# Splitting the queries as whole tiles: rows moved by DMA, the sink's column on ScalarE

## The chip, the cores and the metric

The kernel runs on one core of one Trainium2 chip. The metric is the device time of one execution in microseconds, the median of the runs shown. The engines are TensorE (PE, with its weight loads PEld), VectorE (DVE), ScalarE (ACT), GpSimd (POOL) and SyncE (SP), whose queue issues the DMAs.

## The reference, cut to what matters

Two layers of a hybrid block on 1024 tokens of width 1024. Each layer: RMSNorm; one projection to queries (16 heads of 64), keys and values (2 heads of 64), the two inputs of a convolution and two gates; attention with a window of 128 and learned sinks; a causal depthwise convolution of width 31 with LayerNorm; a gated merge and an output projection; then a SwiGLU feed-forward block. All in float32. The part that the change touches:

```
q = partial_rope(rmsnorm(q, q_norm), cos, sin)      # per head of 64
s = einsum('bnqkgd,bnskd->bnkgqs', qb, kb) * scale  # blocks of 128 queries, 256 keys
m = max(max(s), sink);  p = exp(s - m)
p = p / (sum(p) + exp(sink - m));  o = p @ vb
```

## The kernel before, in words

Everything is kept transposed, channels on partitions and the 1024 tokens along the row. A float32 product is made of three products of reduced-precision parts (F32R): a value x is split into a high part (a cast by ScalarE) and a low part (x minus the high part, by VectorE or GpSimd), and high x high, high x low and low x high are summed in PSUM (`mm3`, line 236). Weights are loaded by SP (`fetch`, L125), cast by ACT (L133) and subtracted by POOL (L134).

In each layer `INPROJ` lists 34 column tiles of the input projection; each takes eight steps of six matmuls, and after every step `tick()` runs the events that are due by then. So attention, the convolution's taps (L496 on VectorE) and the normalisations are laid between the projection's matmuls at fixed steps. The order of PE and, in this part, of DVE is the order in which the program writes its instructions; that of ACT, POOL and SP is chosen by the framework's planner from a model of times, and every engine then works its queue in order.

A query tile holds a pair of heads, head 0 on partitions 0 to 63 and head 1 on 64 to 127. `queries` (L581) evicts it to `q32`, squares it for the norm, and rotates it: `rope` has four small DMAs that shift rows into `rot`, POOL multiplies, DVE adds (L400). `split`, seven steps after the projection, then fills two tiles `qs[0]` and `qs[1]`, one per head, both 128 partitions high: the head's high part on its own 64 partitions, its low part on the other 64. As a key tile `kh` holds the same key rows on both halves, one matmul of 128 rows multiplies high and low part of a head at once. The high halves are two ACT copies (L609), the low halves two DVE subtracts (L613), which read one half of the partitions and write the other.

Sixteen steps after the first query tile the attention units begin, one per six steps: unit (i, j) takes pair i and two blocks of queries. `unit_s` (L622) makes the scores in the PSUM tile `S` (one buffer; L633, L634), puts the sink's column beside them (POOL copy L636 of `sr`, which DVE makes in L599), and copies the rest by ACT (L638); `top` masks (DVE L643, L645), takes the maximum (L649, L651) and the exponentials (ACT L653); `norm` divides (L658, L660). `unit_t` transposes on PE (L669), `masks` selects on POOL (L681, L684), `unit_o` multiplies with the values in the PSUM tile `po` (L699), which the head norm (L391, L394) uses too. PE can write `S` again when L638 and L645 have read it, and `po` when L394 or L711 have.

Tiles tagged `t4` share four buffers of 128x1024: `q32`, `sqh`, the convolution's inputs, the gates.

Of the kernel before, what the change touches and what calls it, by code (L numbers as in the profile page):

```python
# [12 lines left out]
F32 = mybir.dt.float32  # L13
F32R = mybir.dt.float32r
U32 = mybir.dt.uint32
AF = mybir.ActivationFunctionType
ALU = mybir.AluOpType
# [4 lines left out]
P = 128  # L22
# [5 lines left out]
HD = 64  # L28
# [24 lines left out]
def trunk(ctx, tc, xT, win, wcv, wout, wgu, wdn, vecs, cosT, sinT, outT):  # L53
    nc = tc.nc

    def pool(name, bufs=1, space=None, stack=None, side=None):
        kw = dict(name=name, bufs=bufs, reuse_waits="tile")
        if side is not None:
            kw["side"] = side
        if space is not None:  # L60
            kw["space"] = space
        if space is DRAM:
            kw.pop("reuse_waits")
        return (stack or ctx).enter_context(tc.tile_pool(**kw))
# [136 lines left out]
    def next_p():  # L201
        ahead(PAHEAD)
        return pieces.pop(0)


    clock = [0]
# [3 lines left out]
    def at(when, fn):  # L210
        heapq.heappush(events, (when, next(serial), fn))

    def after(n, fn):
        at(clock[0] + n, fn)
# [4 lines left out]
    def when_free(bank, n, fn):  # L219
        def go():  # L220
            if bank in busy:
                after(0.25, go)
            else:
                fn()
        after(n, go)
# [41 lines left out]
    def t4(name):  # L267
        return tp.tile([P, T], F32, tag="t4", bufs=T4, name=name)
# [52 lines left out]
    for l in range(DEPTH):  # L321
        vl = vec[l]

        def V(c, n=1):
            return vl[:, c:c + n]
# [54 lines left out]
        def rope(src):  # L380
            for h in range(2):
                o = h * HD
                nc.sync.dma_start(rot[o:o + 8], src[o + 8:o + 16])
                nc.sync.dma_start(rot[o + 8:o + 16], src[o:o + 8])
            nc.gpsimd.tensor_tensor(out=src, in0=src, in1=ct, op=ALU.mult)
            nc.gpsimd.tensor_tensor(out=rot, in0=rot, in1=st_, op=ALU.mult)

        def headnorm(sq, f):
            pss = ps_o("pssh")
            for b in range(NB):  # L390
                nc.tensor.matmul(pss[:, 2 * b:2 * b + 2], sq[:, b * P:(b + 1) * P], blk1,  # L391
                                 start=True, stop=True)
            ssb = sm.tile([P, NB, 2], F32, tag="ssb", name="ssb")
            nc.vector.tensor_tensor(out=ssb, in0=pss[:, 0:16].rearrange("p (b h) -> p b h", h=2),  # L394
                                    in1=e64.unsqueeze(2).broadcast_to([P, NB, 2]), op=ALU.add)
            nc.gpsimd.tensor_tensor(out=f, in0=ssb.rearrange("p b h -> p (b h)"), in1=mhalf, op=ALU.pow)
            return ssb

        def rope_add(src):
            nc.vector.tensor_tensor(out=src, in0=src, in1=rot, op=ALU.add)  # L400
# [178 lines left out]
        qready = {}  # L579

        def queries(i, ps):  # L581
            q32 = t4("q32")
            nc.scalar.activation(q32, ps, AF.Copy, scale=V(V_GQ))
            sq = t4("sqh")
            nc.scalar.activation(sq, ps, AF.Square)
            rope(q32)
            fq = sm.tile([P, 16], F32, tag="fq", bufs=3, name="fq")
            nfq = sm.tile([P, 16], F32, tag="nfq", bufs=3, name="nfq")
            sr = sm.tile([P, NB, 2], F32, tag="sr", bufs=3, name="sr")
            qs = [ap_.tile([P, T], F32R, tag="qs", bufs=QSB, name=f"qs{h}") for h in range(2)]  # L590

            def norm():
                ssb = headnorm(sq, fq)

                def finish():
                    nc.vector.tensor_scalar(out=nfq, in0=fq, scalar1=-1.0, scalar2=None, op0=ALU.mult)
                    nc.vector.tensor_tensor(out=sr.rearrange("p b h -> p (b h)"),
                                            in0=ssb.rearrange("p b h -> p (b h)"), in1=fq, op=ALU.mult)
                    nc.vector.tensor_tensor(  # L599
                        out=sr, in0=sr,  # L600
                        in1=V(V_SK + 2 * i, 2).unsqueeze(1).broadcast_to([P, NB, 2]), op=ALU.mult)
                after(5, finish)

            def split():
                rope_add(q32)
                for h in range(2):
                    hi = slice(h * HD, (h + 1) * HD)
                    lo = slice((1 - h) * HD, (2 - h) * HD)
                    nc.scalar.copy(qs[h][hi], q32[hi])  # L609
                for h in range(2):  # L610
                    hi = slice(h * HD, (h + 1) * HD)
                    lo = slice((1 - h) * HD, (2 - h) * HD)
                    after(1.5 + h, lambda hi=hi, lo=lo, h=h: nc.vector.tensor_tensor(  # L613
                        out=qs[h][lo], in0=q32[hi], in1=qs[h][hi].bitcast(F32), op=ALU.subtract))
            when_free('po', QN, norm)
            after(QSP, split)
            at(clock[0] + QSP + 3.2, lambda: qready.update({i: (fq, nfq, sr, qs)}))


        Av = {}  # L620
# [1 line left out]
        def unit_s(i, j):  # L622
            fq, nfq, sr, qs = qready[i]
            hk = i // 4
            if j == 0:
                Av[i] = ap_.tile([P, T], F32, tag="A", bufs=AB, name="A")
            S = psm.tile([P, 4, 2 * P], F32, tag="S", bufs=1, name="S")
            for n in range(4):
                b, h = 2 * j + n // 2, n % 2
                qb = qs[h][:, b * P:(b + 1) * P]  # L630
                c0 = P if b == 0 else 0
                ks = slice(b * P - P + c0, (b + 1) * P)
                nc.tensor.matmul(S[:, n, c0:], qb, kh[hk][:, ks], start=True, stop=False)  # L633
                nc.tensor.matmul(S[:, n, c0:], qb, kl[hk][:, ks], start=False, stop=True)  # L634
            sc = ap_.tile([P, 4, P + 1], F32, tag="sc", bufs=SCB, name="sc")
            nc.gpsimd.tensor_copy(sc[:, :, P], sr[:, 2 * j:2 * j + 2].rearrange("p b h -> p (b h)"))  # L636
            f0 = 2 if j == 0 else 0
            nc.scalar.copy(sc[:, f0:, 0:P], S[:, f0:, P:])  # L638
            den = sm.tile([P, 4], F32, tag="den", bufs=3, name="den")

            def top():
                if j == 0:
                    nc.vector.tensor_tensor(out=sc[:, 0:2, 0:P], in0=S[:, 0:2, P:],  # L643
                                            in1=mneg.unsqueeze(1).broadcast_to([P, 2, P]), op=ALU.add)
                nc.vector.copy_predicated(  # L645
                    sc[:, f0:, 0:P], mprev.bitcast(U32).unsqueeze(1).broadcast_to([P, 4 - f0, P]),
                    S[:, f0:, 0:P])
                mx = sm.tile([P, 4], F32, tag="mx", name="mx")
                nc.vector.tensor_reduce(out=mx, in_=sc, axis=AX.X, op=ALU.max)  # L649
                nm = sm.tile([P, 4], F32, tag="nm", name="nm")  # L650
                nc.vector.tensor_tensor(out=nm, in0=mx, in1=nfq[:, 4 * j:4 * j + 4], op=ALU.mult)  # L651
                for n in range(4):
                    nc.scalar.activation(sc[:, n], sc[:, n], AF.Exp, bias=nm[:, n:n + 1],  # L653
                                         scale=fq[:, 4 * j + n:4 * j + n + 1], accum_out=den[:, n:n + 1])

            def norm():
                ri = sm.tile([P, 4], F32, tag="ri", name="ri")
                nc.vector.reciprocal(ri, den)  # L658
                for n in range(4):
                    nc.scalar.activation(sc[:, n, 0:P], sc[:, n, 0:P], AF.Copy, scale=ri[:, n:n + 1])  # L660
            after(T1, top)
            after(T2, norm)
            when_free('pT', TD, lambda: unit_t(i, j, sc))

        def unit_t(i, j, sc):
            busy.add('pT')
            pt = ps_pT("pT").rearrange("p (n q) -> p n q", n=4)
            for n in range(4):
                nc.tensor.transpose(pt[:, n], sc[:, n, 0:P], ident)  # L669
            ph = ap_.tile([P, 4, P], F32R, tag="ph", bufs=1, name="ph")  # L670
            nc.scalar.copy(ph, pt)
            pl = ap_.tile([P, 4, P], F32R, tag="pl", bufs=1, name="pl")
            after(0.6, lambda: masks(i, j, pt, ph, pl))
# [276 lines left out]
        for f in FORD[:NCL]:  # L950
# [4 lines left out]
            for m in range(2):  # L955
                bs = [bank(), bank()]
                held.append(bs)
                for kk in range(2):
                    a = next_p()
# [11 lines left out]
        fq = pool("fq", 1, None, fst)  # L971
# [120 lines left out]
        for n, (name, _, _) in enumerate(DOWN):  # L1092
# [3 lines left out]
            for p in range(NG - fl):  # L1096
                w, a = next_p(), next_p()
# [49 lines left out]
QSP = 7  # L1147
# [72 lines left out]
```

## Time and profile before

| what | value |
|---|---|
| time, median of 3 runs | 2714.76 us (2712.35 to 2716.32) |
| profiled execution | 2710.93 us |
| its span, first to last instruction | 2709.2 us |
| PE busy | 2585.2 us, 95% |
| PE weight loads busy | 2112.5 us, 78% |
| DVE busy | 1876.9 us, 69% |
| ACT busy | 1196.4 us, 44% |
| POOL busy | 1654.0 us, 61% |
| mean granted PE clock | 0.979 of full speed |

The profile is of one execution. "Busy" is a union over the whole span, and stages with different limits are mixed in it; the stages have to be read one by one. A duration of an instruction includes time in which it has begun but cannot go on. Idle time of an engine is put down to the instruction whose end released it.

### The profile page before, as it was taken

To read this page: it belongs to the slowest core of one execution; us is meant where nothing else is said; L and a number is where in the kernel's file an instruction comes from. 1 tells how busy PE (TensorE), PEld (TensorE's weight loads), DVE (VectorE), ACT (ScalarE), POOL (GpSimd) and SP (SyncE) were. 2 spreads that over 40 slices of the span, in tenths; PEclk is the share of its full clock that TensorE was granted. 3 is DMA by queue.
4 is the path that set the end of the run, shared out by engine and by line. 5 is a ranking of instruction groups with operands and counts; after the bars stand their busy time and mean duration, and the time that the engine had idled before them with its cause. 6 is when DMAs were issued, how large, how long until landed. Compare 5 with 4: busy or idle time off the path is not lost. (4 is left out here: it accounts for less than half of the span.)

```text
span 2709.2 us, 33260 instructions
## 1 busy us (share of the span) xinstructions
PE 2585.2 (95%) x11736; PEld 2112.5 (78%) x11736; DVE 1876.9 (69%) x2053; ACT 1196.4 (44%) x2251; POOL 1654.0 (61%) x1092
## 2 busy tenths in 40 slices
PE   7898898999999999999999989899999999999999
PEld 5777777888787888878877767778887788888887
DVE  6689999652468777855637999995616668778344
ACT  2266566843432323344523665668325222223443
POOL 7368787535356777764535778785252677767544
PEclk8999999999999999999999999999999999999999
DMA  3111111375244454476711111114752444455666
GB/s 129 42 51 34 57 64 51 140 264 215 86 165 149 170 179 156 160 276 218 239 57 43 41 57 49 59 63 156 251 202 97 175 167 145 163 179 191 223 224 210
DMA packets 132359, 379.06 MB, mean 140 GB/s; under 512 B 15136, under 2 KB 15392, under 8 KB 132192
## 3 DMA queue, kind: packets, MB, share of 16 engines
q1 hardware_dynamic: 132048, 376.85, 40.6%
q8 instruction: 92, 1.51, 0.2%
q14 instruction: 75, 0.61, 0.1%
q10 hardware_dynamic: 144, 0.09, 0.0%
HBM read 259.17 MB, written 115.34 MB: 138 GB/s over the span
## 5 line engine op out<-in xcount | busy, mean ns | idle before, releaser
L151 POOL TENSOR_TENSOR plo<-fraw,phi 128x512 fp32r<-128x512 f32 x290 | 423.0, 1467 | 229.2 <-ACT phi L149 214.7
L151 POOL TENSOR_TENSOR plo<-fs,phi 128x512 fp32r<-128x512 f32 x160 | 264.3, 1663 | 253.5 <-ACT phi L149 241.7
L496 DVE SCALAR_TENSOR_TENSOR y<-a,vec,y 128x1024 f32<-128x1024 f32 x240 | 405.7, 1690 | 4.0
L134 POOL TENSOR_TENSOR wl<-raw,wh 128x1024 fp32r<-128x1024 f32 (+1 forms) x100 | 252.4, 2525 | 241.7 <-PE ps L242 196.6
L149 ACT CAST phi<-fraw 128x512 fp32r<-128x512 f32 x444 | 257.6, 618 | 246.4 <-POOL plo L151 131.8
L242 PE MATMUL ps<-hx,wh 128*128 128x512 f32 x1056 | 349.1, 412 | 7.3 <-ACT hx L283 7.3
L242 PE MATMUL ps<-hx,wl 128*128 128x512 f32 x1056 | 335.8, 399 | 4.4 <-POOL wl L134 4.4
L242 PE MATMUL ps<-lx,wh 128*128 128x512 f32 x1056 | 338.0, 401 | 0.8 <-DVE lx L284 0.8
L149 ACT CAST phi<-fs 128x512 fp32r<-128x512 f32 x160 | 95.4, 620 | 534.3 <-DVE fs L164 529.1
L151 DVE TENSOR_TENSOR plo<-fraw,phi 128x512 fp32r<-128x512 f32 x154 | 133.6, 873 | 187.8 <-ACT phi L149 185.5
L847 PE MATMUL b<-plo,phi 128*128 128x512 f32 x616 | 240.8, 391 | 3.9 <-DVE plo L151 3.6
L242 PEld LDWEIGHTS ps<-hx,wl 128*128 128x128 f32 x1056 | 204.8, 194 | 50.0 <-POOL wl L134 4.8
L242 PEld LDWEIGHTS ps<-lx,wh 128*128 128x128 f32 x1056 | 206.1, 195 | 47.9 <-DVE lx L284 1.6
L847 PE MATMUL b<-phi,plo 128*128 128x512 f32 x616 | 239.8, 389 | 0.0
L847 PE MATMUL b<-phi 128*128 128x512 f32 x616 | 239.7, 389 | 0.0
L242 PEld LDWEIGHTS ps<-hx,wh 128*128 128x128 f32 x1056 | 195.6, 197 | 42.9 <-ACT hx L283 7.3
L653 ACT ACTIVATE sc<-sc,nm,fq 128x129 f32<-128x129 f32 x256 | 123.7, 486 | 118.0 <-DVE nm L651 117.6
L133 ACT CAST wh<-raw 128x1024 fp32r<-128x1024 f32 (+1 forms) x100 | 98.2, 982 | 166.0 <-PE ps L242 128.3
L915 POOL TENSOR_TENSOR g<-g,u 128x512 f32<-128x512 f32 (+1 forms) x84 | 129.4, 1558 | 31.9 <-DVE u L968 25.5
L911 DVE TENSOR_TENSOR g<-g 128x512 f32<-128x512 f32 x88 | 102.0, 1159 | 65.7 <-POOL g L915 42.5
L847 PEld LDWEIGHTS b<-plo,phi 128*128 128x128 f32 x616 | 115.6, 188 | 31.6 <-DVE plo L151 7.6
L847 PEld LDWEIGHTS b<-phi 128*128 128x128 f32 x616 | 115.6, 188 | 24.2
(254 smaller groups left out, 6219.2 us busy)
## 6 DMA issues: line engine op xcount, KB each, us to landing
fraw<-wgu SPq DMA_DIRECT2D x88, 512.0 KB
raw<-win SPq DMA_DIRECT2D x68, 512.0 KB
act<-g SPq DMA_DIRECT2D x44, 512.0 KB
dw<-wdn SPq DMA_DIRECT2D x44, 512.0 KB
td<-g SPq DMA_DIRECT2D x44, 512.0 KB
sd<-dw SPq DMA_DIRECT2D x44, 512.0 KB
fraw<-sd SPq DMA_DIRECT2D x88, 256.0 KB
fraw<-td SPq DMA_DIRECT2D x88, 256.0 KB
```

The lines of the kernel that those rows point to most:

```text
L133: nc.scalar.copy(wh, raw)
L134: nc.gpsimd.tensor_tensor(out=wl, in0=raw, in1=wh.bitcast(F32), op=ALU.subtract)
L149: nc.scalar.copy(hi, src)
L151: (eng or nc.gpsimd).tensor_tensor(out=lo, in0=src, in1=hi.bitcast(F32), op=ALU.subtract)
L242: nc.tensor.matmul(ps[:, sl], a[:, wc], b[:, sl], start=first and j == 0, stop=last and j == 2)
L496: nc.vector.scalar_tensor_tensor(out=y, in0=a[:, j:j + T], scalar=V(w0 + j), in1=y, op0=ALU.mult, op1=ALU.add)
L653: nc.scalar.activation(sc[:, n], sc[:, n], AF.Exp, bias=nm[:, n:n + 1], scale=fq[:, 4 * j + n:4 * j + n + 1], accum_out=den[:, n:n + 1])
L847: nc.tensor.matmul(ps, w[:, ai * P:(ai + 1) * P], x, start=first and j == 0, stop=last and j == 2, skip_group_check=True)
L911: nc.vector.tensor_tensor(out=o, in0=x, in1=y, op=ALU.subtract)
L915: nc.gpsimd.tensor_tensor(out=g[:, sl], in0=g[:, sl], in1=u[:, sl], op=ALU.mult)
```

## The change

The high part of a pair is now one ACT copy of the whole 128x1024 tile into a new `t4` tile `qhi`, and the low part one DVE subtract of the whole tile, written over `q32`. Four DMAs on SP's queue, each of 64 rows of 4 KB from SBUF to SBUF, then bring the rows to `qs[0]` and `qs[1]`: per head the high rows to its own half and the low rows to the other. The subtract stands where the first of the two stood (1.5 steps after `split`); the second is gone. The step at which a pair is entered as ready is put later; it sets no order. Apart from that the sink's column (L636) is copied by ACT instead of POOL.

```
             def split():
                 rope_add(q32)
-                for h in range(2):
-                    ...
-                    nc.scalar.copy(qs[h][hi], q32[hi])
-                for h in range(2):
-                    ...
-                    after(1.5 + h, lambda hi=hi, lo=lo, h=h: nc.vector.tensor_tensor(
-                        out=qs[h][lo], in0=q32[hi], in1=qs[h][hi].bitcast(F32), op=ALU.subtract))
+                hi = t4("qhi")
+                nc.scalar.copy(hi.bitcast(F32R), q32)
+
+                def low():
+                    nc.vector.tensor_tensor(out=q32.bitcast(F32R), in0=q32, in1=hi, op=ALU.subtract)
+
+                    for h in range(2):
+                        r, o = (slice(a * HD, (a + 1) * HD) for a in (h, 1 - h))
+                        q = qs[h].bitcast(F32)
+                        nc.sync.dma_start(q[r], hi[r])
+                        nc.sync.dma_start(q[o], q32[r])
+                after(1.5, low)
             when_free('po', QN, norm)
             after(QSP, split)
-            at(clock[0] + QSP + 3.2, lambda: qready.update({i: (fq, nfq, sr, qs)}))
+            at(clock[0] + QSP + 5, lambda: qready.update({i: (fq, nfq, sr, qs)}))
...
-            nc.gpsimd.tensor_copy(sc[:, :, P], sr[:, 2 * j:2 * j + 2].rearrange("p b h -> p (b h)"))
+            nc.scalar.copy(sc[:, :, P], sr[:, 2 * j:2 * j + 2].rearrange("p b h -> p (b h)"))
```

## Rows read from the trace of the kernel before

**Rows 1.** Stages: start:end and length, busy us of PE, PEld, DVE, ACT, POOL; clock, DMA.
```profile
185.00:240.00 55.00, 49.73 (x246) 42.01 (x247) 53.73 (x60) 34.12 (x78) 43.13 (x28) 0.91 0.14 41
600.00:720.00 120.00, 115.64 (x507) 94.40 (x505) 39.81 (x39) 37.18 (x46) 49.98 (x24) 1.00 0.42 156
```
**Rows 2.** Waits of PE: line, whom it waited for, total us, times, longest.
```profile
PE S L633 <- DVE sc L645: 38.5, 16, 5.0
PE po L699 <- DVE ssb L394: 27.1, 8, 4.7
```
**Rows 3.** Timeline of PE in layer 0: start, duration, instruction, [idle before, releaser].
```profile
118.33 0.33 PE L633 MATMUL S<-kh,qs 128*128 128x128 f32 x1
...
132.51 0.55 PE L633 MATMUL S<-kh,qs 128*128 128x256 f32 x1 [5.04 <-DVE sc L645]
...
169.82 0.33 PE L633 MATMUL S<-kh,qs 128*128 128x128 f32 x1 [1.65 <-DVE sc L645]
...
185.54 0.36 PE L633 MATMUL S<-kh,qs 128*128 128x256 f32 x1 [3.67 <-DVE sc L645]
...
471.40 0.55 PE L699 MATMUL po<-mo,vv 128*128 128x256 f32 x1 [4.60 <-DVE ssb L394]
```
**Rows 4.** Timeline of DVE, first and second pair of heads.
```profile
113.00 2.70 DVE L613 TENSOR_TENSOR qs<-q,qs 64x1024 fp32r<-64x1024 f32 x1
...
117.05 1.22 DVE L613 TENSOR_TENSOR qs<-q,qs 64x1024 fp32r<-64x1024 f32 x1
...
161.44 4.54 DVE L613 TENSOR_TENSOR qs<-q,qs 64x1024 fp32r<-64x1024 f32 x2
...
169.04 0.72 DVE L645 COPY_PREDICATED sc<-mprev,S 128x512 f32<-128x512 uint32 x1
...
183.90 0.81 DVE L492 TENSOR_SCALAR y<-a,vec 128x1024 f32<-128x1024 f32 x1 [3.99 <-DMA yd<-y]
```
**Rows 5.** Groups by line and form: count, busy us, mean ns, idle before them.
```profile
L613 DVE TENSOR_TENSOR qs<-q,qs 64x1024 fp32r<-64x1024 f32 x32 | 74.5, 2327 | 0.9
...
L636 POOL COPY sc<-sr 128x4 f32<-128x4 f32 x64 | 53.2, 833 | 68.9 <-PE pT L669 41.1 <-DVE sr L599 27.7
...
L653 ACT ACTIVATION_READ_ACCUMULATOR sc<-sc,nm,fq 128x1 f32 x256 | 47.9, 187 | 0.0
...
L609 ACT CAST qs<-q 64x1024 fp32r<-64x1024 f32 x32 | 33.5, 1046 | 25.3 <-DVE q L400 25.0
...
L400 DVE TENSOR_TENSOR q<-q,rot 128x1024 f32<-128x1024 f32 x16 | 19.5, 1217 | 2.5 <-POOL rot L386 2.5
```
**Rows 6.** Stage table for line 613 alone, third pair: DVE busy, clock, DMA.
```profile
205.00:230.00 25.00, 6.64 (x2) 0.87 0.07 22
```
**Rows 7.** Timeline of POOL, first and second pair.
```profile
102.68 2.40 POOL L385 TENSOR_TENSOR q<-q,ct 128x1024 f32<-128x1024 f32 x1 [3.91 <-DMA rot<-q]
...
160.30 3.37 POOL L134 TENSOR_TENSOR wl<-raw,wh 128x1024 fp32r<-128x1024 f32 x1
...
167.99 1.18 POOL L636 COPY sc<-sr 128x4 f32<-128x4 f32 x1 [1.51 <-DVE sr L599]
```
**Rows 8.** Waits of POOL before the sink's column.
```profile
POOL sc L636 <- PE pT L669: 41.1, 10, 9.1
...
POOL sc L636 <- DVE sr L599: 27.7, 16, 4.2
```
**Rows 9.** Timeline of SP's queue, 95 to 240 us: start and time of each issue.
```profile
99.60 0.62 SPq L384 DMA_DIRECT2D rot<-q  x1
...
164.08 0.43 SPq L767 DMA_DIRECT2D sB<-g  x1
178.86 0.33 SPq L125 DMA_DIRECT2D raw<-win  x1
179.94 0.33 SPq L503 DMA_DIRECT2D yd<-y  x1
```
**Rows 10.** Chain that ended last: start, us, what (a load of 256 KB).
```profile
2679.55 6.26 DMA x<-xs
```

More of the change, by code (lines that the diff above doesn't have):

```diff
@@ L605, in split @@
                 rope_add(q32)
-                for h in range(2):
-                    hi = slice(h * HD, (h + 1) * HD)
-                    lo = slice((1 - h) * HD, (2 - h) * HD)
-                    nc.scalar.copy(qs[h][hi], q32[hi])
-                for h in range(2):
-                    hi = slice(h * HD, (h + 1) * HD)
-                    lo = slice((1 - h) * HD, (2 - h) * HD)
-                    after(1.5 + h, lambda hi=hi, lo=lo, h=h: nc.vector.tensor_tensor(
-                        out=qs[h][lo], in0=q32[hi], in1=qs[h][hi].bitcast(F32), op=ALU.subtract))
+                hi = t4("qhi")
[8 more added lines that the diff above has]
+                after(1.5, low)
             when_free('po', QN, norm)
             after(QSP, split)
-            at(clock[0] + QSP + 3.2, lambda: qready.update({i: (fq, nfq, sr, qs)}))
+            at(clock[0] + QSP + 5, lambda: qready.update({i: (fq, nfq, sr, qs)}))
         Av = {}
```

## The prediction

> **What bounds the kernel now.** I read the table of stages first. In the stages of layer 0 with attention (185 to 240 us) DVE is busy 53.73 of 55 us, PE only 49.73 and at a granted clock of 0.91; in the block after it (600 to 720) PE has 115.64 of 120 and DVE a third [rows 1]. So the projections with attention, to about 480 us and in the like stretch of layer 1, are bound by DVE, the rest mostly by PE. The list of PE's waits agrees: 38.5 us in 16 waits for the copy that empties the score bank S (L645), 27.1 us in 8 for the tiny L394 that empties the other bank [rows 2]. Neither op is long; each stands at the end of a full DVE queue. PE's timeline shows where: 5.04 us at 132.51, 1.65 at 169.82, 3.67 at 185.54, the last of the layer 4.60 at 471.40 [rows 3]. DVE's timeline of the pair of heads before 169.82 shows the queue: two L613 subtracts from 161.44 on, small ops and taps, L645 ending at 169.76, after which PE starts at once; the only idle stretch is 3.99 us at 183.90, for a store that DVE's own last tap had triggered, so it moves with DVE [rows 4]. In such a stretch a microsecond less on DVE is a microsecond less in the kernel, as long as PE still waits.
>
> **The change, part by part.**
>
> *Half subtracts.* 32 subtracts of 64x1024 take 74.5 us, 2.33 on average [rows 5]; 16 of 128x1024 take their place. The number of partitions costs DVE no time: the rope's add of 128x1024 takes 1.22 us on average (L400) [rows 5], and so does a half subtract at its shortest (117.05) [rows 4]. So the new one takes what one old one took, and one falls away per pair. Its price lies between two ends, neither below nothing, as it leaves a full queue. Alone it is 1.22 us; beside a large POOL op it is 2.70 (113.00), and in one pair the two took 6.64, or 3.3 each [rows 4, 6]. The first of a pair runs into POOL's wl subtract (160.30 to 163.67 beside 161.44) [rows 4, 7]; the new one sits at that same place in DVE's order and keeps that collision. I take 1.22 for the one removed, as in most pairs: where it took more, POOL's op will meet the tap behind it. The last pair of a layer pays nothing, since its subtract stands behind the layer's last wait for DVE at 471.40 [rows 3]. 14 pairs x 1.22 = 17.1 us; the upper end is the whole difference, 16 x (4.65 - 2.70 to 3.3), about 22 to 31 us.
>
> *High parts.* ACT's two half copies (1.05 us each [rows 5]) become one: 16.8 us less on ACT, which has 34.12 of 55 us busy [rows 1]. Worth 0; the copy still ends before DVE comes to the subtract.
>
> *The sink's column.* 64 POOL copies go, 53.2 us, 0.83 each [rows 5], up to 1.18 for four columns [rows 7], more waiting than work. DVE gets at most a start earlier on a few ops, or meets POOL's next op sooner: between -3 and +3, I take 0. On ACT each costs between 0.19 (its accumulator read, one column) and 1.05 (L609) [rows 5]; I take 0.2, as four columns are nearest to one: 13 us, less than the 16.8 that left, and at 1.05 the 50 more would still fit into ACT's idle 21 of 55. POOL idled 41.1 us before this copy for PE's transposes and 27.7 for DVE's sr [rows 8]; in ACT's order these waits now stand in front of exponentials, weight casts and evictions. I take 0, since L638, which follows on ACT, fills the same buffer and has the same wait, and sr is done before the unit's matmuls; if not, it is the second rival.
>
> *The four transfers.* 64 in all, 256 KB each, SBUF to SBUF, on SP's queue. The trace has no such transfer. Issue: 0.43 us for a store (164.08), 0.62 for the small shifts of rot (99.60) [rows 9], so 4 x 0.43 to 0.62 = 1.7 to 2.5 us of SP per pair. From issue to use: rot, 32 KB, issued at 99.60, is read at 102.68: 3.1 us; the 512 KB store yd issued at 179.94 releases DVE at 183.90: 4.0; the worst of 256 KB, in the crowded last stage, is 6.26 [rows 4, 7, 9, 10]. I take 4.0, because the stage is as quiet as at yd, and 0.4 for one issue ahead of it, as the two high parts can leave while DVE still subtracts: 4.4 us from the subtract's end to qs (3.1 to 8.8 at the ends).
>
> Where does that fall? Pair 1: the new subtract ends at 161.44 + 4.54 - 1.22 = 164.76, qs lands at 169.2. S comes free at 169.76 - 1.22 = 168.5. So PE starts at 169.2 and not 169.82, with half of the gain, and the rest is had at 185.54, where DVE alone decides and its queue has run 1.22 earlier all along. Pair 0 has no room: its subtract ends at 115.70, qs lands at 120.1, and the second head was read at 118.33 [rows 3]; PE loses some 2 us there. The wait of 5.04 at 132.51 takes them in, since DVE sets its end and has a full queue until then; without that cover they would cost 2 x 2 us.
>
> What is behind the new waits: SP, in order, holds the four issues until DVE is done. The weight load behind them (or ahead: it left just before 164.08, released by POOL's wl at 163.67) may be 1 to 3 us later; the load after it leaves only at 178.86, so a projection lies in between [rows 7, 9]. The t4 tiles: one more of four is held from the copy to the landing; beside it are q32, at times the held ur and one gate tile, and sqh is free by then. Four fit; nothing is charged.
>
> [...]
>
> Sum: -17 us. The profiled execution took 2710.93 us (span 2709.2), 3.8 less than the median of 2714.76; the same step off the median gives 2698.
>
> **Rivals.**
> 1. More: the removed subtract is worth its average, and POOL, freer, gets in DVE's way less: -25 to -33 us, some 2686. For it: 6.64 us in the pair at 205 to 230 [rows 6]. Against it: POOL's large ops all remain, and each stops some DVE op.
> 2. No change: the sink copy at the head of ACT's queue. If a third of the 68.8 us that POOL idled before it [rows 8] passes through the exponentials to DVE and PE, 23 us come and the 17 are gone: 2715 to 2721. For it: ACT is in order and its exponentials stand between two DVE ops of each unit. Against it: the same wait stands at L638 already.
> 3. Slower: the way from subtract over SP to qs becomes what each pair waits for. Its room from the subtract's end to PE's old start is 169.82 - 164.76 = 5.1 us in pair 1, and 3.67 more before DVE's next release [rows 3]. From about 9 us nothing is left, and each further microsecond is paid in about 15 pairs. The place where that can happen is SP: transfers ordered behind the next weight load (178.86 [rows 9]) would land at about 183.9, 19 us after the subtract: 10 x 15 = +150, 2865; at 11 us it would be 2 x 15 = +30, 2745. Against it: the subtract is ready 1 us after one load and 14 before the next, and a wrong guess of order by a few microseconds does no harm.
>
> **How the numbers follow.** Main case (-8 to -24) 0.60, rival 1 0.10, rival 2 0.15, rival 3 0.15. What can be told from no change here is about 0.2%, 5.4 us. Faster is the first two, with a little of the main case lost to no change: 0.68; same 0.17; slower 0.15. The likeliest time is 2698 (its own range 2690 to 2707); the range of 8 in 10 reaches from 2681, rival 1's lower end, to 2720, near rival 2's upper and leaves out rival 3.
>
> **What would show it.** Right: 16 DVE subtracts of 128x1024 with a mean near 3 us where there were 32 of 2.33; PE's waits for L645 and L394 down from 65.6 us by 15 to 20; at the first unit of a pair PE waits for a DMA into qs, 4 to 5 us after the subtract, longest (about 2 us) in the first pair of each layer; POOL about 53 us less busy. Wrong: waits for qs that sum to more than the waits for DVE lose; qs issued behind a weight load; ACT idle before the sink's copy and DVE idle before L658; a DVE that stays as busy because its taps became longer; any t4 writer waiting for a landing.

## The result: 15 us less, and where they come from

The kernel after takes 2697.96 us (median of 6 runs, 2693.72 to 2704.77) against 2713.0 for the kernel before (6 runs) on the same chip: a ratio of 0.9947, 95% interval [0.9932, 0.9962]. A second measurement of the same kernel (the first experiment) gave 2698.07, ratio 0.9955 [0.9942, 0.9969]. The forecast was 2698. The first profile of the kernel after caught its longest run (2704.77 us, mean granted clock 0.975); the readings below are from the profile of that second measurement, an execution of 2696.70 us (span 2695.0, clock 0.982), where nothing else is said. In after, the subtract is L610, the high copy L607, the transfers L615 and L616, the score matmuls L636 and L637, the sink's copy L639, the masked copy L648, the masks L684 and L687, `po` L702.

The pages of after, busy time of each engine, first and second profile:

```profile
PE 2588.6 (96%) x11736; PEld 2118.2 (78%) x11736; DVE 1843.6 (68%) x2037; ACT 1190.6 (44%) x2299; POOL 1601.5 (59%) x1028
...
PE 2575.1 (96%) x11736; PEld 2106.0 (78%) x11736; DVE 1852.3 (69%) x2037; ACT 1190.8 (44%) x2299; POOL 1602.4 (59%) x1028
```

The stage table of after, the stretches of [rows 1] first, then three short ones at the end of layer 0's attention:

```profile
185.00:240.00 55.00, 49.29 (x252) 41.04 (x252) 53.57 (x61) 35.62 (x88) 41.60 (x26) 0.95 0.21 61
600.00:720.00 120.00, 115.64 (x508) 94.66 (x507) 37.30 (x37) 35.20 (x44) 51.27 (x24) 0.99 0.42 156
...
471.60:477.10 5.50, 1.50 (x6) 1.01 (x7) 5.46 (x5) 2.69 (x3) 5.50 (x4) 0.70 0.60 177
477.90:480.50 2.60, 2.60 (x9) 2.02 (x8) 2.53 (x4) 1.38 (x4) 1.70 (x2) 0.50 0.96 318
```

And one stretch of the kernel before, just after its own last wait for DVE:

```profile
472.50:475.00 2.50, 2.50 (x9) 2.02 (x9) 2.36 (x5) 2.04 (x6) 2.50 (x1) 0.50 0.00 0
```

DVE is as full as before in such a stage (53.57 of 55 us); what shrank is the stage. The waits of PE in after, which answer to [rows 2]:

```profile
PE po L702 <- POOL ph L687: 14.9, 8, 3.0
PE S L636 <- DVE sc L648: 13.5, 9, 2.7
PE po L702 <- DVE ssb L394: 11.5, 8, 2.2
PE S L636 <- DMA qs<-q: 10.9, 10, 3.9
PE po L702 <- POOL pl L687: 9.5, 9, 1.2
```

The two waits for DVE fell from 65.6 to 25.0 us, 40.6 less. Two others came: 10.9 for the transfers into `qs`, and 24.4 for POOL's masks of the previous block, where the same two rows of before read 1.3 (ph) and 4.5 (pl):

```profile
PE po L699 <- POOL pl L684: 4.5, 4, 1.2
...
PE po L699 <- POOL ph L684: 1.3, 1, 1.3
```

So 40.6 - 10.9 - 18.6 = 11.1 us of these waits are gone. That is not the whole account of the 14.2 us between the two spans (2709.2 and 2695.0). Smaller waits grew, and all of PE's idle time, the span less the busy time, fell by only 4.2 us, from 124.0 to 119.9. The other 10.0 us are busy time: the same 11736 matmuls took 2575.1 us and not 2585.2, at a mean granted clock of 0.982 against 0.979 (0.95 against 0.91 in the stage from 185 to 240 us). How much comes by which way differs between executions: the first profile of after has 114.4 us idle and 2588.6 busy, at 0.975. PE's timeline in layer 0, the instructions of [rows 3] in order, and two more:

```profile
119.38 0.30 PE L636 MATMUL S<-kh,qs 128*128 128x128 f32 x1 [0.55 <-DMA qs<-q]
...
120.53 0.33 PE L636 MATMUL S<-kh,qs 128*128 128x128 f32 x1 [0.73 <-DMA qs<-q]
...
130.79 0.36 PE L636 MATMUL S<-kh,qs 128*128 128x256 f32 x1 [1.11 <-DVE sc L648]
...
171.32 0.44 PE L636 MATMUL S<-kh,qs 128*128 128x128 f32 x1 [3.87 <-DMA qs<-q]
...
185.70 0.36 PE L636 MATMUL S<-kh,qs 128*128 128x256 f32 x1 [0.70 <-DVE sc L648]
...
460.98 0.35 PE L702 MATMUL po<-mo,vv 128*128 128x256 f32 x1 [1.29 <-DVE ssb L394]
...
475.11 0.58 PE L702 MATMUL po<-ph,vv 128*128 128x256 f32 x1 [3.01 <-POOL ph L687]
476.68 0.58 PE L702 MATMUL po<-pl,vv 128*128 128x256 f32 x1 [0.99 <-POOL pl L687]
```

Read the starts against those of before. The layer's last wait for DVE ends at 460.98 and not at 471.40: 10.4 us won. Soon after, PE stands 3.01 and 0.99 us for masks, in a unit that before ran through at once (its first matmul of `po` there is at 483.90), and has only 5.7 us left when the stage ends. The stage table shows what followed there: PE had been busy 1.50 of the 5.50 us up to 477.10, and from 477.90 to 480.50 the granted clock is 0.50. The kernel before shows the like behind its own wait of 4.60 us, at 0.50 from 472.50 to 475.00, so the lead first grows from 10.4 to 12.4 us; the unit that waits for the masks then takes 6.7 of it. Layer 1 goes the same way: 6.3 us ahead at its start, 17.1 at its last wait for DVE, 12.6 at the end of the stage.

### The profile page after: what moved, and what is told of

It reads as the page before. It is cut to its first block, busy times and chain, and to the rows that moved or that the text cites. A ratio compares the mean times of both kernels' runs of the same rounds, so it can differ in the third digit from the quotient of the medians.

```text
span 2703.0 us, 33316 instructions
## 1 busy us (share of the span) xinstructions
PE 2588.6 (96%) x11736; PEld 2118.2 (78%) x11736; DVE 1843.6 (68%) x2037; ACT 1190.6 (44%) x2299; POOL 1601.5 (59%) x1028
## 4 chain that ended last, share of the span: by engine, by line
PE 64%; DVE 21%; DMA 4%; POOL 4%; issue 3%; ACT 2%; SPq 1%; DVEq 0%; ACTq 0%; POOLq 0%
PE b L850 40%; PE ps L242 20%; DVE y L496 9%; DVE mx L652 1%; DVE sc L648 1%; DVE q L610 1%; DVE acc L295 1%; DVE A L714 1%; DMA qs<-q 1%; PE po L702 1%; POOL q L385 1%; DVE pl L679 1%; DVE g L724 1%; DMA x<-xs 1%; POOL wl L134 1%
## 5 line engine op out<-in xcount | busy, mean ns | idle before, releaser
L134 POOL TENSOR_TENSOR wl<-raw,wh 128x1024 fp32r<-128x1024 f32 (+1 forms) x100 | 241.0, 2411 | 292.2 <-PE ps L242 250.3
L850 PEld LDWEIGHTS b<-phi 128*128 128x128 f32 x616 | 116.0, 188 | 24.3
```

Source lines behind the costliest of these rows:

```text
L134: nc.gpsimd.tensor_tensor(out=wl, in0=raw, in1=wh.bitcast(F32), op=ALU.subtract)
L850: nc.tensor.matmul(ps, w[:, ai * P:(ai + 1) * P], x, start=first and j == 0, stop=last and j == 2, skip_group_check=True)
```

## The experiments

All were timed against the kernel before on the same chip. "Interval" is the 95% interval of the ratio to it.

**The same kernel again (`e1_after_again`).**

> The changed kernel once more, as the measure for the three beside it. Both theories: 2693 to 2702 us, 12 to 18 below the kernel before. In its profile the first unit of five or six pairs per layer waits for ScalarE's copy of the sink's column, which waits for DVE's sr: about 64 us of ScalarE idle, and PE waits some 27 us in all for POOL's masks of ph and pl, where the kernel before has 6.

2698.07 us, interval [0.9942, 0.9969]. The gain stands, and this is the base of what follows.

**Rows alone, sink's column back on POOL (`e2_rows_only`).**

```
-  nc.scalar.copy(sc[:, :, P], sr[...])
+  nc.gpsimd.tensor_copy(sc[:, :, P], sr[...])
```

> Whole tiles and DMA as in the changed kernel, the sink's column on POOL as before. Theory A (the gain is the DVE subtract that fell away, and the move of the sink's column gives some of it back, because at the head of ScalarE's queue it waits for sr and holds the cast of ph that PE's next product needs): faster than the changed kernel, 2683 to 2692 us, PE's waits for POOL's masks back to about 6 us, PE's gain of about 8 us per layer at the head norm of the last pair kept to the layer's end. Theory B (the gain comes from POOL, freed of 64 copies; the rows alone bring little): slower than the changed kernel, 2704 to 2713.

2698.47 us, [0.994, 0.9965]: the same as after, so both theories on the sink's column fall. PE's largest waits are after's too:

```profile
PE po L702 <- POOL ph L687: 15.0, 6, 3.2
PE S L636 <- DVE sc L648: 13.7, 8, 2.8
```

This is the net of a different schedule, though: the 16 subtracts take 50.4 us here and 41.1 in after, and in the second pair of layer 0 the first score matmul comes 5.9 us after the subtract and not 10.7.

**Sink's column alone (`e3_sink_only`).** The kernel before with L636 copied by ACT, the edit of `e2_rows_only` the other way round, and nothing else.

> The kernel before with the sink's column on ScalarE and nothing else. Theory A: no faster than the kernel before, 2713 to 2725 us, with ScalarE idle before the copy until DVE's sr and PE waiting for POOL's masks. Theory B: most of the gain, 2697 to 2706.

2711.42 us, [0.9992, 1.0011]: nothing. That the copy heads ACT's queue is visible all the same. The waits of ACT in after:

```profile
ACT sc L639 <- DVE sr L599: 71.3, 16, 5.4
ACT sc L656 <- DVE nm L654: 66.6, 41, 4.1
...
ACT sc L639 <- PE pT L672: 39.6, 25, 2.7
```

110.9 us stand in front of the sink's copy, but ACT's wait for nm in front of the exponentials is 66.6 now where it was 117.6: ACT waits in another place, partly for the same DVE. Others wait for ACT more than before, POOL in front of its masks 114.3 us where it was 29.1, DVE in front of its reciprocal 35.4 where it was 24.2; PE does so for 5.5 us (4.2 before), and e3 shows no cost in time.

**Transfers kept, subtract cut in two again (`e4_two_halves`).**

```
-  nc.vector.tensor_tensor(out=q32.bitcast(F32R), in0=q32, in1=hi, op=ALU.subtract)
+  for a in range(2):
+      s = slice(a * HD, (a + 1) * HD)
+      nc.vector.tensor_tensor(out=q32.bitcast(F32R)[s], in0=q32[s], in1=hi[s], op=ALU.subtract)
```

> The changed kernel with the whole-tile subtract written as two subtracts of 64 partitions, so that DVE has the 32 half subtracts of the kernel before; high copy, DMAs and the sink's column as in the changed kernel. Theory A: the 17 us are gone, 2711 to 2720 us. Theory B, or any in which the number of DVE instructions doesn't decide: 2694 to 2702 as the changed kernel.

2717.64 us, [1.0013, 1.003]: 19.6 more than after, and 6.2 more than before. So one subtract for two is worth about 20 us as these two kernels stand, and the way over the transfers costs about 6 net. Neither is the price of one thing alone: POOL's order differs too (PE waits 10.0 us for its masks here and 24.4 in after), and the half subtracts take less here than in before (65.1 us against 74.5 [rows 5]). The groups of this kernel and PE's waits:

```profile
L612 DVE TENSOR_TENSOR q<-q,qhi 64x1024 fp32r<-64x1024 f32 x32 | 65.1, 2035 | 0.5
```

```profile
PE po L704 <- DVE ssb L394: 26.4, 8, 4.6
PE S L638 <- DVE sc L650: 21.2, 13, 4.3
PE S L638 <- DMA qs<-q: 14.0, 9, 3.9
```

The wait for ssb is back at 26.4; that for the transfers stays.

**A third half subtract in the kernel before (`e7_extra_sub`).**

```
+  after(2.5, lambda: nc.vector.tensor_tensor(
+      out=qs[0][HD:], in0=q32[0:HD], in1=qs[0][0:HD].bitcast(F32), op=ALU.subtract))
```

> The kernel before with a third 64x1024 subtract per pair on DVE (it writes the same numbers again). It measures what one half subtract is worth. By the prediction's term (14 pairs x 1.22 us) 17 us more: about 2730. By the average duration (16 x 2.33) 37 us more: 2750. If DVE isn't what ends the pairs: 2711 to 2716. From putting the second subtract back into the kernel after (19.6 us more) I expect 2728 to 2734.

2734.50 us, [1.007, 1.0096]: 23.1 more, 1.44 for each of 16, at the upper end of what I expected. Here no transfer is involved, so this prices the subtract by itself: between its shortest 1.22 and its mean 2.33 [rows 5], nearer the first.

**A longer way to `qs` (`e8_two_hops`).**

```
   nc.sync.dma_start(q[r], hi[r])
-  nc.sync.dma_start(q[o], q32[r])
+  nc.sync.dma_start(hi[r], q32[r])
+  nc.sync.dma_start(q[o], hi[r])
```

> The kernel after, but each low half is brought to its tile by two transfers in a row (over the rows of the high parts' tile, which are free by then), so the way from the subtract to qs is some 4 to 5 us longer, about 9 us in all. The prediction's third rival put the point from which delay is paid at about 9 us: by it 2698 to 2710. If the way is already what each pair that waits for qs stands on (10 waits in the kernel after), each pays the whole of it: 10 x 4.5 = 45 us, 2740 or more. If it had room to spare everywhere: 2698, and no longer waits for qs in the trace.

2741.55 us, [1.0094, 1.012]: 43.5 more than after, close to the second case. SP's queue and PE's wait in the third pair of this kernel, whose subtract ends at 224.37:

```profile
224.40 1.10 SPq L616 DMA_DIRECT2D qhi<-q  x2
228.23 1.49 SPq L617 DMA_DIRECT2D qs<-qhi  x2
```

```profile
231.35 0.45 PE L637 MATMUL S<-kh,qs 128*128 128x128 f32 x1 [4.08 <-DMA qs<-qhi]
```

From the subtract's end to the pair's first score matmul it is 7.0 us here and 5.6 in after. Summed over the 16 pairs that way grew by 39.0 us, and the kernel by 43.5. It is not simply paid one for one. Counted from the subtract's end, the last hop left SP 69.0 us later in sum, so some 30 us were absorbed before the first matmul, and of the 44.6 us between the two spans PE's idle time is 28.9 and its busy time 15.6, at a mean clock of 0.971 against 0.982. But pairs with a short way pay too: in the eight whose way stayed under 9 us it grew by 23.2 in sum, and the distance from their subtract to the next pair's by 19.0.

**All weight subtracts of POOL behind the masks (`e5_masks_first`, and `e6_masks_first_old` on the kernel before).** What started it is POOL's order at the end of layer 0's attention. First before, then after:

```profile
476.42 0.63 POOL L681 TENSOR_SCALAR_AFFINE_SELECT mo<-pl 128x512 fp32r<-128x512 f32 x1
477.01 1.62 POOL L684 TENSOR_SCALAR_AFFINE_SELECT ph<-ph 128x512 fp32r<-128x512 f32 x1
478.59 0.63 POOL L684 TENSOR_SCALAR_AFFINE_SELECT pl<-pl 128x512 fp32r<-128x512 f32 x1
479.19 2.41 POOL L134 TENSOR_TENSOR wl<-raw,wh 128x1024 fp32r<-128x1024 f32 x1
```

```profile
470.53 0.63 POOL L684 TENSOR_SCALAR_AFFINE_SELECT mo<-pl 128x512 fp32r<-128x512 f32 x1
471.13 2.35 POOL L134 TENSOR_TENSOR wl<-raw,wh 128x1024 fp32r<-128x1024 f32 x1
473.43 1.62 POOL L687 TENSOR_SCALAR_AFFINE_SELECT ph<-ph 128x512 fp32r<-128x512 f32 x1
475.01 1.61 POOL L687 TENSOR_SCALAR_AFFINE_SELECT pl<-pl 128x512 fp32r<-128x512 f32 x1
```

The planner has put the weights' subtract between the masks. In after it stands so in front of the masks ph and pl in three pairs of each layer, in before and in `e4_two_halves` in one.

```
+  def late(low=low):                 # low: POOL's subtract into wl
+      with tc.issue_after(masked[1]):    # the last mask recorded so far
+          low()
+  after(5.5, late)                   # ... in the stages with attention alone
```

> The kernel after, but POOL's subtract for the next weight tile (L134) is always queued behind the masks of the probabilities, never between the own block's masks and the previous block's. In the kernel after PE waits 24.4 us for those masks (po for ph 14.9, for pl 9.5), longest 3.0 us where the weight's subtract stands ahead of them. Theory (what DVE gains, some 11 us a layer, is given back by half because of POOL's order): these waits fall to 10 us or less and the time by 6 to 12 us, to 2686 to 2692. Rival 1 (the masks are late because the casts before them, on ACT and DVE, are late): waits for POOL stay above 18 us, time 2695 to 2701. Rival 2 (the weight tiles come late instead): PE's wait for wl grows from 7.4 us to over 15, time 2698 to 2710.

> The kernel before, with the same edit to POOL's order. There PE waited 5.8 us for the masks (pl 4.5, ph 1.3). Theory (the late masks came with the change's new order): at most those few us can be won, 2706 to 2714. Rival (the order is worth as much in the kernel before, and has nothing to do with the change): 2699 to 2705.

2712.19 us, [0.999, 1.0007], and 2755.12, [1.014, 1.0167]. PE's waits in e5, then in e6:

```profile
PE ps L251 <- POOL wl L135: 40.7, 15, 4.5
...
PE po L712 <- POOL pl L696: 5.7, 5, 1.2
...
PE po L712 <- POOL ph L696: 4.7, 4, 1.2
```

```profile
PE ps L251 <- POOL wl L135: 63.7, 17, 6.0
```

The masks came in time (24.4 down to 10.4), but the weights late (40.7 us of waiting; after has 7.4 there), as the second rival said, with a time just above its range; in e6 the miss was complete, as I had not counted that there. As a test of the order it was too blunt.

**Only the six that stand between the masks (`e9_masks_some`, `e11_masks_some`).**

```
+  if given[1] not in (22, 25, 28, 72, 75, 78): low()
+  else: after(1.5, late)             # late as above
```

> The kernel after with six of the weight subtracts on POOL moved: only those that its order puts between the own block's masks and the previous block's masks (three a layer, in the pairs 5 to 7), and only to behind these masks, some 3 us later each; nothing else stands elsewhere. In the kernel after the six units lose 4.2, 2.3 and 4.0 us in each layer there. Theory (this order gives back what DVE gains late in the layer, and putting all weight subtracts late failed only because the weights of the other pairs came late): PE's waits for ph and pl fall from 24.4 us to about 8, its wait for wl stays under 12, and the time falls by 8 to 14 us, to 2684 to 2690. Rival 1 (DVE's wait takes their place at once): waits for sc and ssb grow by as much, 2694 to 2700. Rival 2 (the weights come late here too): wait for wl over 15, 2700 or more.

> The same, and in the second pair of each layer the weight load that stood between the high and the low rows on SP's queue, and held the low rows 4.8 us after the subtract until POOL released its buffer, goes behind them. If the way from the subtract to qs is paid one for one (as the two transfers in a row showed: 43 us for about 41 us of later first units), PE's gap of 4.3 and 2.5 us there goes and the kernel gains 3 to 6 us over the one with the six subtracts moved alone. If DVE's waits in the following units (1.1 and 3.1 us) take it up: 0 to 2 us. The load leaves about 1 us later, which should cost nothing.

In these two a step of the feed-forward stage was recorded too early as well, which changes what it computes, so their times (2743.13 and 2738.71 us) say nothing; their attention stages do, and gave the numbers for the next two, which are without that edit.

> The kernel after with only the six weight subtracts of POOL moved behind the masks, and the feed-forward stage as in the kernel after (in e9_masks_some a step of it, the block sums of the activations, was recorded 2.5 planner steps too early as well, which changed what it computes and cost some 26 us in layer 0 there). In e9's two stages with attention PE stood 9.6 us ahead of the kernel before at the end of the stage in layer 0 (kernel after: 5.7) and won 8.7 us in layer 1's (kernel after: 6.3). Theory (POOL's order gave that back): 6 us less than the kernel after, 2689 to 2694, waits for ph and pl under 9 us in all. Rival (DVE's waits take it up, or it is lost again in the stages behind): 2695 to 2700.

2689.98 us, [0.9899, 0.9928]: 8.1 below after, and the intervals don't touch (9.2 if each is taken against the kernel before on its own chip, 22.6 and 13.4 below it). Its waits of PE:

```profile
PE S L645 <- DVE sc L657: 17.1, 13, 2.7
PE S L645 <- DMA qs<-q: 12.1, 11, 3.9
...
PE po L711 <- DVE ssb L403: 6.9, 6, 2.2
PE po L711 <- POOL pl L696: 6.2, 7, 1.2
...
PE po L711 <- POOL ph L696: 1.2, 2, 0.6
```

The wait for ph is 1.2 us and that for pl 6.2, together 7.4 where after has 24.4, and DVE's (24.0 in all) took up none of it. PE, ACT and DVE have the same order as in after; so POOL's order had given back 8 us. Two limits: one of the three pairs a layer had the subtract there in before as well, so not all of the 8 came with the change; and DVE's subtracts in these six pairs fell from 2.9 to 3.3 us to 1.5 to 1.7, so how much of the 8 came through the masks and how much through DVE isn't split.

**And the low rows ahead of a weight load (`e12_both`).** In the second pair of each layer SP stood on a weight load whose buffer POOL still held. SP's queue of after there; the subtract had ended at 160.60:

```profile
164.46 0.33 SPq L125 DMA_DIRECT2D raw<-win  x1
...
165.36 1.81 SPq L616 DMA_DIRECT2D qs<-q  x2
```

```
+  if given[2] in (12, 62):               # that load, once a layer; 3 steps later
+      with tc.issue_after(masked[1]):    # here: the pair's last transfer
+          nc.sync.dma_start(raw, src)
+  ...
```

> The same as e11_masks_some, with the weight load of the second pair of each layer behind the low rows on SP's queue, and the feed-forward stage as in the kernel after. By e10's stages with attention (10.6 us ahead at the end of layer 0's, 12.1 won in layer 1's, so 1.1 and 3.4 more than in e9): 2 to 6 us below e11_masks_some, 2684 to 2690. Rival (the wait for sc that took the place of that for qs, 4.0 us in the second unit of that pair, eats it): within 1.5 us of e11.

2686.27 us, [0.9883, 0.9914]: 3.7 below e11 by the medians, which is not clear of noise (the intervals overlap; PE's idle time fell by 4.8 us between the two profiles), and 26.3 below before. SP's queue and PE's next wait in that pair:

```profile
161.26 1.50 SPq L631 DMA_DIRECT2D qs<-q  x2
165.10 0.34 SPq L131 DMA_DIRECT2D raw<-win  x1
```

```profile
182.87 0.55 PE L651 MATMUL S<-kh,qs 128*128 128x256 f32 x1 [3.59 <-DVE sc L663]
```

The rows leave 4 us earlier, and the pair's first score matmul starts at 167.97 and not at 171.32. In the next unit DVE is late by 3.59 us where it was 0.70, yet that matmul starts at 182.87 and not at 185.70: 2.8 of the 3.4 us are kept. This is the best version.

## Why the prediction was right, step by step

**The bound: right.** DVE ends the pairs of the attention stages. Putting the second subtract back cost 20 us, adding a third to the kernel before cost 23, and PE's waits for DVE fell from 65.6 to 25.0 us, twice the 15 to 20 forecast, as other waits took part of their place.

**Half subtracts: right mechanism, size too small.** Sixteen subtracts take 2.57 us on average, not near 3, and the slowest pair's one takes 3.44 where two took 6.64 [rows 6]:

```profile
L610 DVE TENSOR_TENSOR q<-q,qhi 128x1024 fp32r<-128x1024 f32 x16 | 41.1, 2569 | 0.0
...
L639 ACT COPY sc<-sr 128x4 f32<-128x4 f32 x64 | 12.2, 194 | 111.0 <-DVE sr L599 71.3 <-PE pT L672 39.6
```

```profile
205.00:230.00 25.00, 3.44 (x1) 0.93 0.23 65
```

The term was 17.1; it measured 19.6 (e4, with POOL's new order against it) and 23.1 (e7). The pairs of half subtracts in e4 sum to 65.1 us and the whole ones here to 41.1, 1.50 less per pair. In before the second of a pair took 1.22 us in eleven of 16 pairs and 24.7 in all, so 1.54 on average. Nor did the one that stays keep its collision everywhere, as I had supposed: the first ones took 49.7 us in before, and five of the whole ones take only 1.21 to 1.65.

**The sink's column and the high parts: right, 0.** The copy takes 0.194 us on ACT (0.2 taken), POOL is 52.5 us less busy (1654.0 to 1601.5), and e2 and e3 put the move at 0 within about 3 us. Rival 2 falls: the wait at ACT's head is there and costs nothing that these runs can tell.

**The four transfers: the landing right, their cost wrong.** Two issues take 1.10 us. In the first pair the subtract ends at 116.0, the second head is read at 120.53: 4.5 us, 4.4 forecast. The high rows were out of the way as supposed: their two issues ran from 112.06 to 113.24. But I charged nothing for the transfers, and e4 shows 6 us.

**Pair 1: wrong.** I had qs land at 169.2, ahead of S. The low rows were queued behind the weight load, the place that rival 3 names, and left 4.8 us after the subtract; PE started at 171.32, 1.5 later than before and not 0.6 earlier. The prediction said that the load might be 1 to 3 us late, and that a wrong order of a few microseconds did no harm; e12 puts the harm at 3.7 us for two pairs, by the medians.

**Rival 3's break-even: wrong.** From 9 us on, it said, delay is paid. In e8 eight pairs had a way of 6.2 to 8.9 us where it was 3.4 to 5.6, and 19.0 of these 23.2 us came back as distance to the next pair. The 3.67 us of DVE lateness that I had counted as room behind PE's start is little room: the masked copy, the maximum and all that follows on DVE wait for this unit's scores, so a late S delays the same in-order queue that sets the next release. (That reason is read from the code's order; the runs show the price: in e12 an S earlier by 3.4 us made the next release earlier by 2.8.)

**Not in the prediction: POOL.** I had the masks nowhere. PE, earlier by 10 us, met POOL's masks, and POOL's order had changed: some 8 us lost (e11), by three pairs a layer of which two were new. The replan came with the single subtract; `e4_two_halves`, with the transfers but two subtracts, has the old order at this place. Why the planner chose so wasn't tried.

So the main mechanism was right, but that the sum came out at 2698 to the microsecond is luck: two errors cancel. The kernels timed make three steps. The transfers with two half subtracts cost 6.2 us (before to e4); one subtract for two, with the masks in order, gives 27.7 (e4 to e11, which ran on another chip); the masks out of order cost 8.1 (e11 to after). Together that is -13.4. The term of the subtract was 17.1, and it measured 27.7 with POOL's order left out and 19.6 with it in; the 6.2 and the 8.1 were set at nothing. The steps depend on each other, as the subtracts too are shorter in e11 (34.0 us in all, 41.1 in after), and the last few microseconds are not split further. Nor did the prediction have a term for PE's clock, by which a part of the gain arrives in the second profile (0.982 against 0.979, with 10.0 us less of busy time).

## What to carry to other kernels

When an engine's queue gets shorter, look at once for the engine that stood a little behind it, and at the order that the planner now gives to the others: here a 2.4 us weight subtract, put in front of a mask in three pairs of a layer, cost some 8 us. Slack read off a wait is little slack if the waiting engine's own next work depends on the late operand. A transfer on SP's queue cost its landing (4.5 us from the subtract to the use in the first pair) plus what stood in front of it (4.8 us behind a weight load in the second), so compare the order of issues in the new trace, not only their durations.

## What the runs showed of the hardware

How long DVE's subtract took went with what POOL ran beside it, and POOL's ops stretched as well. The subtract of 128x1024 takes 1.21 us at 269.93, with POOL idle; 1.65 at 158.95, beside two masks of 128x512, which take 1.61 each there and 0.63 just before; and 3.44 at 214.0, beside a weight subtract and an add of 128x1024 that take 3.46 and 3.38 (about 2.4 at their shortest). An edit shows it as well: in e5, where POOL's weight subtracts come later, the same 16 subtracts take 24.6 us and not 41.1.

```profile
L619 DVE TENSOR_TENSOR q<-q,qhi 128x1024 fp32r<-128x1024 f32 x16 | 24.6, 1539 | 0.0
```

So a DVE op can weigh more than its shortest duration: the half subtract, 1.22 us at its shortest in before, cost 1.44 for each of the 16 that were added (e7).

And PE's 4.0 us of waiting at 475 us were followed by slower matmuls: the six from 477.91 on, at a granted clock of 0.50, took 2.56 us where the six from 468.20 to 469.59 took 1.39. In before six took 1.36 (477.11 to 478.47), in a stretch at 1.00 (477.00 to 480.00).
